# A macaron encoder block on one core: the feed-forward activations turned by DMA in 16-bit halves instead of by TensorE

## The chip, the cores and the metric

The kernel runs on one core of a Trainium2 chip. The metric is device time in microseconds of one execution of the whole program; lower is better. Inputs and weights lie in the chip's memory in a layout packed for the kernel, and packing is not timed.

## The reference, cut to what matters

```python
# x (1, 256, 2048), d_ff = 5632, everything float32
x = x + 0.5 * swiglu(rmsnorm(x, ffn1_norm), w_gate1, w_up1, w_down1)
h = rmsnorm(x, mix_norm)
z = h @ w_in                                   # 2048 -> 7168: u | v | gate logits
a = pool_branch(u); b = conv_branch(v)         # pooling and 31-tap convolution, each -> 2048
x = x + (sigmoid(g_a) * a + sigmoid(g_b) * b) @ w_out
x = x + 0.5 * swiglu(rmsnorm(x, ffn2_norm), w_gate2, w_up2, w_down2)
out = rmsnorm(x, final_norm)

def swiglu(h, w_gate, w_up, w_down):
    return (silu(h @ w_gate) * (h @ w_up)) @ w_down
```

The change touches only the product silu(...) * (...) of the two feed-forwards, on its way into `w_down`.

## The kernel before

All 256 tokens stay on the chip as two tiles `X` of 128 tokens by 2048. Weights stream from memory once, in pieces of 128 rows by 1024 columns (`raw`, five buffers), issued on SP's queue.

**Words in two parts.** TensorE multiplies in a shortened float32 format, so every operand is held as a high part and a low part: `hi_lo` lets ScalarE cast to the high part (`wh`, L153) and VectorE subtract it for the low part (`wl`, L155). A product is three matmuls: high by high, high weights' low part, low activations (L256).

**Chunks.** The work is one list, `stream`, of chunks. A chunk is two pieces of weights (256 rows of the inner dimension), and a `Unit` is the run of chunks that fills one set of accumulators: 8 chunks for a unit of 2048 rows. A normal chunk is 24 matmuls of 128x512. Chunks 0 and 2 of most feed-forward units (`SEVEN`) use a seven-product form instead: 21 matmuls, for which VectorE first forms sums of weights (`sum`, L193), ScalarE casts them (`exth`, L153) and VectorE subtracts (`extl`, L155).

**The order.** No scheduler reorders anything: `run` walks the list. At chunk i it issues the loads of chunk i+2, casts the weights of chunk i+1 (`split_chunk`), calls what was put down for this place with `at(i, ...)`, and then issues chunk i's matmuls (`run_chunk`). Each engine executes its own instructions in that order. Converted weights have buffers for two chunks.

**The feed-forward.** A gate unit multiplies by 512 columns of `w_gate` and 512 of `w_up` together; there are 11 such units in a feed-forward. After units 4 and 8 come the units of `w_down` for the four hidden blocks finished so far, and at the end those for the last three. When a gate unit's last chunk is issued, `gate_done_seven` (for unit 0 `gate_done`) adds the partial results on VectorE (`part`, L413), applies silu on ScalarE (L414) and multiplies on VectorE (`h`, L418): two tiles of 128 tokens by 512 hidden columns.

`w_down` needs the hidden columns on the partitions. So `put` has TensorE turn four 128x128 squares of h against an identity into one bank of PSUM (`transposes`, L343), and `hi_lo` makes the high and low parts of `ht` out of the bank. It is called twice for a unit, in chunks 4 and 5 of the next unit, with two 128-column blocks each time; `gate_early` puts it down there, `rest_of_hidden` after the last unit. For the chunks in the seven-product form a copy `hy` (L389) feeds `e_forms`, which makes differences of hidden blocks (`hE`).

Of the kernel before, what the change touches and what calls it, by code (L numbers as in the profile page):

```python
# [7 lines left out]

F32 = mybir.dt.float32
F32R = mybir.dt.float32r  # L10
AF = mybir.ActivationFunctionType
ALU = mybir.AluOpType

P = 128
D = 2048
T = 256
NT = T // P
# [8 lines left out]
C = 512  # L26
W2 = 2 * C
KD = D // P
# [12 lines left out]
GROUP = 4  # L41
# [40 lines left out]
def encoder_kernel(ctx: ExitStack, tc: tile.TileContext, x, xT, vecs, rows, pool_m,  # L82
# [30 lines left out]
    def at(i, fn):  # L113

        side.setdefault(i, []).append(fn)
# [12 lines left out]
    def add_unit(u):  # L128
        for cc in range(u.k // 2):
            stream.append((u, cc))  # L130
# [21 lines left out]
    def hi_lo(src, h, l=None):  # L152
        nc.scalar.copy(out=h, in_=src)  # L153
        if l is not None:
            nc.vector.tensor_tensor(out=l, in0=src, in1=h.bitcast(F32), op=ALU.subtract)  # L155
        return h, l
# [136 lines left out]
    def hidden(pool, name):  # L293

        return [tuple(block(pool, f"h{s}{u}", F32R, f"{name}{s}{u}") for s in "hl") for u in range(GROUP)]

# [5 lines left out]
    def e_forms(dst, even, odd):  # L302

        e = stg.tile([P, 4, P], F32, tag="sg", name=f"e{Pos.now}")
        a11, a21, a12, a22 = even[:, :P], even[:, P:], odd[:, :P], odd[:, P:]
        for n, (a, b) in enumerate(((a11, a21), (a21, a22), (a11, e[:, 1, :]), (a12, e[:, 2, :]))):
            nc.vector.tensor_tensor(out=e[:, n, :], in0=a, in1=b, op=ALU.subtract)
        hi_lo(e, *dst)
# [29 lines left out]
    def transposes(src_of, n, name, b=None):  # L338

        b = bank(name) if b is None else b  # L340
        for j in range(n):
            for t in range(NT):
                nc.tensor.transpose(out=b[:, j * T + t * P: j * T + (t + 1) * P],  # L343
                                    in_=src_of(j, t), identity=ident)
        return b
# [24 lines left out]
    def open_ffn(stack, n):  # L370

        pool = ffn["pool"] = stack.enter_context(tc.tile_pool(name=f"ffn{n}", bufs=1))
        ffn["ht"] = hidden(pool, f"ht{n}")
        ffn["hE"] = e_tiles(pool, "h", n)
        ffn["t0"], ffn["t1"] = (pool.tile([P, 2, C], F32, tag=f"part{t}", name=f"part{n}_{t}") for t in range(NT))

    def ffn_units(w_g, w_d, xt, xE, rs, residual_done, tail=None):
        waiting = []

        def hidden_lhs(k, t):  # L380
            return tuple(h[:, k % 4, t * P:(t + 1) * P] for h in ffn["ht"][k // 4])

        def put(u, hs, k0, b=None):
            b = transposes(lambda j, t: hs[t][:, (k0 + j) * P:(k0 + j + 1) * P], 2, f"hT{Pos.now}_{k0}", b)
            hi_lo(b.rearrange("p (q t) -> p q t", q=2), *(h[:, k0:k0 + 2, :] for h in ffn["ht"][u % GROUP]))
            c = (u % GROUP) * 2 + k0 // 2
            if c in SEVEN:
                y = stg.tile([P, 2, T], F32, tag="sg", name=f"hy{Pos.now}_{k0}")
                nc.scalar.copy(out=y, in_=b.rearrange("p (q t) -> p q t", q=2))  # L389
                e_forms(ffn["hE"][c], y[:, 0, :], y[:, 1, :])  # L390

        def hidden_tile(t):
            return stg.tile([P, C], F32, tag="h", name=f"h{Pos.now}_{t}")

        def gate_done(u):
            def done(acc):
                hs = []
                for t in range(NT):
                    sg = stg.tile([P, C], F32, tag="sg", name=f"sg{Pos.now}_{t}")
                    h = hidden_tile(t)  # L400
                    nc.scalar.activation(sg, acc[t][:, 0, :], AF.Silu, scale=rs[:, t:t + 1])  # L401
                    nc.vector.scalar_tensor_tensor(out=h, in0=acc[t][:, 1, :], scalar=rs[:, t:t + 1],
                                                   in1=sg, op0=ALU.mult, op1=ALU.mult)
                    hs.append(h)
                waiting.append((u, hs))
            return done

        def gate_done_seven(u):
            def done(acc):
                hs = []  # L410
                for t in range(NT):
                    z = ffn[f"t{t}"]
                    nc.vector.tensor_tensor(out=z, in0=acc[t], in1=z, op=ALU.add)  # L413
                    nc.scalar.activation(z[:, 0, :], z[:, 0, :], AF.Silu, scale=rs[:, t:t + 1])  # L414
                for t in range(NT):
                    z = ffn[f"t{t}"]
                    h = hidden_tile(t)
                    nc.vector.scalar_tensor_tensor(out=h, in0=z[:, 1, :], scalar=rs[:, t:t + 1],  # L418
                                                   in1=z[:, 0, :], op0=ALU.mult, op1=ALU.mult)
                    hs.append(h)  # L420
                waiting.append((u, hs))
            return done

        def shared_parts():

            z0, z1 = ffn["t0"], ffn["t1"]
            nc.scalar.copy(out=z0[:, 0, :], in_=ps[:, B_P1, :])
            for out, a, b, op in ((z1[:, 1, :], ps[:, B_P6, :], z0[:, 0, :], ALU.subtract),
                                  (z0[:, 1, :], ps[:, B_P5, :], z1[:, 1, :], ALU.add),
                                  (z1[:, 0, :], ps[:, B_P7, :], z1[:, 1, :], ALU.subtract),  # L430
                                  (z1[:, 1, :], z0[:, 1, :], ps[:, B_P7, :], ALU.subtract)):
                nc.vector.tensor_tensor(out=out, in0=a, in1=b, op=op)

        def gate_early():
            shared_parts()
            if waiting:
                u, hs = waiting.pop()
                at(Pos.now + 1, lambda: put(u, hs, 0, ps[:, B_P6, :]))
                at(Pos.now + 2, lambda: put(u, hs, 2, ps[:, B_P1, :]))

        def into_residual(t, half, part):
            xs = X[t][:, half * W2:(half + 1) * W2]
            nc.vector.scalar_tensor_tensor(out=xs, in0=part.rearrange("p a b -> p (a b)"), scalar=0.5, in1=xs,
                                           op0=ALU.mult, op1=ALU.add)

        def down_early(half):
            def early():
                shared_parts()
                for t in range(NT):
                    at(Pos.now + 1 + t, lambda t=t: into_residual(t, half, ffn[f"t{t}"]))  # L450
            return early

        def down_done(half, last):
            def done(acc):
                for t in range(NT):
                    into_residual(t, half, acc[t])
                    if last:
                        squares(t, 2 * half, half * W2, (half + 1) * W2)
                if last:
                    residual_done(half)  # L460
            return done

        def rest_of_hidden():
            u, hs = waiting.pop()
            at(Pos.now + 2, lambda: put(u, hs, 0))
            at(Pos.now + 3, lambda: put(u, hs, 2))

        def add_down(g, k, last):
            for half in range(2):
                if last:  # L470
                    add_unit(Unit(w_d[half], k, hidden_lhs, down_done(half, True), tail if half else None,
                                  k0=g * GROUP * 4, start=None if half else rest_of_hidden))
                else:
                    add_unit(Unit(w_d[half], k, hidden_lhs, down_done(half, False), k0=g * GROUP * 4,
                                  forms=forms_of(hidden_lhs, LateE()), early=down_early(half), seven=SEVEN))

        class LateE:
            def __getitem__(self, c):
                return ffn["hE"][c]

        units = FF // C
        for u in range(units):
            if u:
                add_unit(Unit(w_g[u], KD, lhs_of(xt), gate_done_seven(u), forms=forms_of(lhs_of(xt), xE),
                              early=gate_early, seven=SEVEN, start=(lambda: None) if u == 1 else None))
            else:
                add_unit(Unit(w_g[u], KD, lhs_of(xt), gate_done(u)))
            if u and u % GROUP == 0:
                add_down(u // GROUP - 1, 4 * GROUP, False)
        add_down((units - 1) // GROUP, 4 * (units - (units - 1) // GROUP * GROUP), True)  # L490
# [387 lines left out]
    at(n3 - 1, final_first_half)  # L878


    xr = [block(ffn["pool"], f"xr{j}", F32, f"xr{j}") for j in range(4)]
    start()
    for i in range(PF - 1):
        load(i)
# [124 lines left out]
```

## Time and profile before

| what | value |
|---|---|
| median of 3 runs | 1945.61 us (1945.37 to 1945.71) |
| the profiled execution's own time | 1945.58 us |
| its span in the profile | 1943.8 us |
| granted TensorE clock | 0.999 |
| memory read | 380.28 MB, 197 GB/s over the span |

All rows below come from that one execution. "Busy" is the time in which an engine had an instruction under way. The chain that ended last goes back from the last instruction, at each step to what released it, and says which engine set the end. In rows in order of time the first number is the start in microseconds from the span's start and the second the duration; square brackets hold the engine's idle time before the row and what ended it. ACTq stands for ScalarE's instruction queue issuing a DMA, SPq for SP's.

### The profile page before, as it was taken

What the parts mean: (1) busy time and instruction counts of PE and PEld (TensorE: products, weight loads), DVE (VectorE), ACT (ScalarE), POOL (GpSimd) and SP (SyncE); (2) the same over time, 40 slices, a digit from 0 to 9 for tenths busy, and PEclk for the clock granted to TensorE, in tenths of its full rate; (3) what the DMA queues carried; (4) which work ended last, traced back from release to release, by engine and by line L of the source; (5) the groups of instructions that cost most, each with busy time, mean ns of one, the idle gap of its engine ahead of it and who ended that gap; (6) DMA issues with size and microseconds to landing.
All of it is one profiled execution on the core that took longest, in us unless ns stands there. A gap on an engine that the chain in (4) does not pass through costs nothing.

```text
span 1943.8 us, 23272 instructions
## 1 busy us (share of the span) xinstructions
PE 1931.8 (99%) x8680; PEld 1597.5 (82%) x8680; DVE 1520.0 (78%) x1762; ACT 975.7 (50%) x1117; POOL 11.3 (1%) x22
## 2 busy tenths in 40 slices
PE   9999999999999999999999999999999999999998
PEld 7888888888888888888888888888888888888886
DVE  6888888888888555888888766688888888888855
ACT  6555544554545454454444545455554455554544
POOL 0000000000000000000000000000000000000000
PEclk9999999999999999999999999999999999999999
DMA  8555566655665556566666555555656665566664
GB/s 316 191 183 198 193 216 192 203 190 190 198 204 201 189 188 202 189 200 208 204 206 200 190 184 185 183 194 179 201 196 215 191 199 193 186 201 203 197 194 147
DMA packets 106145, 383.90 MB, mean 198 GB/s; under 512 B 11920, under 2 KB 12176, under 8 KB 105776
## 3 DMA queue, kind: packets, MB, share of 16 engines
q1 hardware_dynamic: 104688, 378.45, 59.2%
q0 software_dynamic: 1056, 3.83, 0.6%
q8 instruction: 68, 1.11, 0.2%
q14 instruction: 45, 0.37, 0.1%
q10 hardware_dynamic: 288, 0.14, 0.0%
HBM read 380.28 MB, written 2.10 MB: 197 GB/s over the span
## 4 chain that ended last, share of the span: by engine, by line
PE 98%; DVE 1%; issue 0%; ACT 0%; DMA 0%; DVEq 0%; POOLq 0%; POOL 0%; ACTq 0%
PE ps L256 82%; PE ps L277 13%; PE ps L343 2%; PE ps L741 0%; DVE wl L155 0%; DMA xr<-in_xT 0%; DVE sum L193 0%; PE ps L716 0%; ACT exth L153 0%; ACT wh L153 0%; DVE extl L155 0%; DVE raw L193 0%; ACT fsq L850 0%; ACT sg L401 0%; PE ps L623 0%
## 5 line engine op out<-in xcount | busy, mean ns | idle before, releaser
L153 ACT CAST wh<-raw 128x1024 fp32r<-128x1024 f32 (+1 forms) x706 | 726.5, 1048 | 710.9 <-PE ps L256 393.9
L155 DVE TENSOR_TENSOR wl<-raw,wh 128x1024 fp32r<-128x1024 f32 (+1 forms) x706 | 844.5, 1218 | 300.4 <-ACT wh L153 297.4
L256 PE MATMUL ps<-wh,xt1h 128*128 128x512 f32 x544 | 170.6, 395 | 1.2 <-ACT wh L153 1.2
L256 PE MATMUL ps<-wh,xt3h 128*128 128x512 f32 x544 | 169.6, 393 | 0.0
L256 PE MATMUL ps<-wl,xt1h 128*128 128x512 f32 x544 | 168.4, 391 | 0.0
L256 PE MATMUL ps<-wh,xt1l 128*128 128x512 f32 x544 | 168.0, 390 | 0.0
L256 PE MATMUL ps<-wl,xt3h 128*128 128x512 f32 x544 | 167.9, 390 | 0.0
L256 PE MATMUL ps<-wh,xt3l 128*128 128x512 f32 x544 | 167.6, 389 | 0.0
L256 PE MATMUL ps<-wh,xt2h 128*128 128x512 f32 x448 | 138.4, 390 | 0.0
L256 PE MATMUL ps<-wl,xt2h 128*128 128x512 f32 x448 | 138.1, 389 | 0.0
L256 PE MATMUL ps<-wh,xt2l 128*128 128x512 f32 x448 | 137.9, 389 | 0.0
L256 PEld LDWEIGHTS ps<-wl,xt1h 128*128 128x128 f32 x544 | 102.6, 189 | 21.9 <-DVE wl L155 0.3
L256 PEld LDWEIGHTS ps<-wh,xt1l 128*128 128x128 f32 x544 | 102.4, 188 | 21.6
L256 PEld LDWEIGHTS ps<-wh,xt3l 128*128 128x128 f32 x544 | 102.1, 188 | 21.7
L256 PEld LDWEIGHTS ps<-wl,xt3h 128*128 128x128 f32 x544 | 102.1, 188 | 21.5
L256 PEld LDWEIGHTS ps<-wh,xt1h 128*128 128x128 f32 x544 | 101.1, 189 | 21.4 <-ACT wh L153 1.7
L155 DVE TENSOR_TENSOR extl<-sum,exth 128x1536 fp32r<-128x1536 f32 x56 | 98.5, 1759 | 25.4 <-ACT exth L153 25.4
L256 PEld LDWEIGHTS ps<-wh,xt3h 128*128 128x128 f32 x544 | 100.5, 188 | 19.5
L256 PEld LDWEIGHTS ps<-wl,xt2h 128*128 128x128 f32 x448 | 84.1, 188 | 17.7
L256 PEld LDWEIGHTS ps<-wh,xt2l 128*128 128x128 f32 x448 | 84.1, 188 | 17.5
L600 DVE SCALAR_TENSOR_TENSOR conv<-gluT,vec,conv 128x241 f32<-128x241 f32 (+14 forms) x240 | 96.9, 471 | 0.0
L256 PEld LDWEIGHTS ps<-wh,xt2h 128*128 128x128 f32 x448 | 83.3, 188 | 16.5
(237 smaller groups left out, 2851.9 us busy)
## 6 DMA issues: line engine op xcount, KB each, us to landing
raw<-in_w_g SPq DMA_DIRECT2D x350, 512.0 KB, 4.2
raw<-in_w_d SPq DMA_DIRECT2D x176, 512.0 KB, 4.0
raw<-in_w_in SPq DMA_DIRECT2D x112, 512.0 KB, 3.9
raw<-in_w_out SPq DMA_DIRECT2D x32, 512.0 KB, 3.5
raw<-in_w_pp SPq DMA_DIRECT2D x16, 512.0 KB, 3.7
raw<-in_w_cp SPq DMA_DIRECT2D x16, 512.0 KB, 3.8
row<-in_rows POOLq DMA_DIRECT2D x7, 512.0 KB, 4.0
X<-in_x SPq DMA_DIRECT2D x2, 1024.0 KB, 8.7
```

Source lines behind the costliest of these rows:

```text
L153: nc.scalar.copy(out=h, in_=src)
L155: nc.vector.tensor_tensor(out=l, in0=src, in1=h.bitcast(F32), op=ALU.subtract)
L256: nc.tensor.matmul(u.acc[t + c if u.tail and t else t][:, c, :], lhsT=a, rhs=b[:, c * C:(c + 1) * C], start=(t, c) not in u.begun, stop=k ...
L277: nc.tensor.matmul(ps[:, b, :], lhsT=x_, rhs=w_, start=where not in u.begun, stop=b < B_11 and cc == u.seven[-1] and n == 2)
L343: nc.tensor.transpose(out=b[:, j * T + t * P: j * T + (t + 1) * P], in_=src_of(j, t), identity=ident)
L600: nc.vector.scalar_tensor_tensor(out=dst, in0=src, scalar=w, in1=dst, op0=ALU.mult, op1=ALU.add)
```

## The change

Each h tile is turned by two steps in place of one. `turn`, in the first chunk of the next unit: ScalarE copies h, seen as 16-bit words, into `halves`, the low halves of all words first and then the high ones, and its queue issues a DMA that transposes the 128x1024 half-words into `turned`, eight squares of 128x128. That is done for both token tiles. `put`, in chunk 4 of the next unit: ScalarE joins the halves again with four copies into `y`, and `hi_lo` works on `y`, all four blocks at once. `e_forms` follows one chunk later. The buffers of `ht` are allocated only once the first unit has run, since `xr`, the transposed input, now lies in some of them.

```diff
+U16 = mybir.dt.uint16
 ...
+        def open_hidden():
+            ffn["ht"] = hidden(ffn["pool"], f"ht{stream.index((first, 0))}")
 ...
-        def put(u, hs, k0, b=None):
-            b = transposes(lambda j, t: hs[t][:, (k0 + j) * P:(k0 + j + 1) * P], 2, f"hT{Pos.now}_{k0}", b)
-            hi_lo(b.rearrange("p (q t) -> p q t", q=2), *(h[:, k0:k0 + 2, :] for h in ffn["ht"][u % GROUP]))
-            c = (u % GROUP) * 2 + k0 // 2
-            if c in SEVEN:
-                y = stg.tile([P, 2, T], F32, tag="sg", name=f"hy{Pos.now}_{k0}")
-                nc.scalar.copy(out=y, in_=b.rearrange("p (q t) -> p q t", q=2))
-                e_forms(ffn["hE"][c], y[:, 0, :], y[:, 1, :])
+        def turn(u, hs):
+            turned = []
+            for t in range(NT):
+                halves = ffn["pool"].tile([P, 2, C], U16, tag=f"halves{t}", name=f"halves{Pos.now}_{t}")
+                nc.scalar.copy(out=halves, in_=hs[t].bitcast(U16).rearrange("p (f w) -> p w f", w=2))
+                z = ffn["pool"].tile([P, 8, P], U16, tag=f"turned{t}", name=f"turned{Pos.now}_{t}")
+                nc.scalar.dma_start_transpose(out=z, in_=halves.rearrange("p w f -> p (w f)"))
+                turned.append(z)
+            waiting.append((u, turned))
+
+        def put(u, turned):
+            y = ffn["pool"].tile([P, 4, T], F32, tag="y", name=f"hy{Pos.now}")
+            whole = y.bitcast(U16).rearrange("p j (t w) -> p w j t", w=2)
+            for t in range(NT):
+                for w in range(2):
+                    nc.scalar.copy(out=whole[:, w, :, t * P:(t + 1) * P], in_=turned[t][:, 4 * w:4 * w + 4, :])
+            hi_lo(y, *ffn["ht"][u % GROUP])
+            for c in SEVEN:
+                if c // 2 == u % GROUP:
+                    q = c % 2 * 2
+                    at(Pos.now + 1, lambda c=c, q=q: e_forms(ffn["hE"][c], y[:, q, :], y[:, q + 1, :]))
 ...
-                waiting.append((u, hs))
+                at(Pos.now + 1, lambda: turn(u, hs))
 ...
-                u, hs = waiting.pop()
-                at(Pos.now + 1, lambda: put(u, hs, 0, ps[:, B_P6, :]))
-                at(Pos.now + 2, lambda: put(u, hs, 2, ps[:, B_P1, :]))
+                u, turned = waiting.pop()
+                at(Pos.now + 1, lambda: put(u, turned))
 ...
         def rest_of_hidden():
-            u, hs = waiting.pop()
-            at(Pos.now + 2, lambda: put(u, hs, 0))
-            at(Pos.now + 3, lambda: put(u, hs, 2))
+            at(Pos.now + 3, lambda: put(*waiting.pop()))
 ...
-    xr = [block(ffn["pool"], f"xr{j}", F32, f"xr{j}") for j in range(4)]
+    xr = [block(ffn["pool"], f"h{x}{j}", F32, f"xr{x}{j}") for j in (2, 3) for x in "hl"]
```

The order of instructions at the three places that matter, in the stretch where unit 2 of the first feed-forward has ended (chunk 23) and unit 3 runs (chunks 24 to 31). The number in a name is the chunk it belongs to. First ScalarE at the start of unit 3, before the change (the two silus of unit 2, the weights of chunk 25, the three casts of chunk 26):

```order
L414 ACTIVATE part1_0_115<-part1_0_115,rstd0_82 128x512
L414 ACTIVATE part1_1_116<-part1_1_116,rstd0_82 128x512
L153 CAST wh25_0_1226<-raw25_0_1169 128x1024
L153 CAST wh25_1_1230<-raw25_1_1171 128x1024
L153 CAST wh26_0_1266<-raw26_0_1222 128x1024
L153 CAST exth26_1264<-sum26_1259 128x1536
L153 CAST wh26_1_1272<-raw26_1_1224 128x1024
```

And now:

```order
L432 ACTIVATE part1_0_107<-part1_0_107,rstd0_82 128x512
L432 ACTIVATE part1_1_108<-part1_1_108,rstd0_82 128x512
L154 CAST wh25_0_1228<-raw25_0_1171 128x1024
L154 CAST wh25_1_1232<-raw25_1_1173 128x1024
L391 COPY halves24_0_1236<-h23_0_1220 128x1024
L393 DMA_TRANSPOSE turned24_0_1238<-halves24_0_1236 128x8x128
L391 COPY halves24_1_1240<-h23_1_1222 128x1024
L393 DMA_TRANSPOSE turned24_1_1242<-halves24_1_1240 128x8x128
L154 CAST wh26_0_1276<-raw26_0_1224 128x1024
L154 CAST exth26_1274<-sum26_1269 128x1536
L154 CAST wh26_1_1282<-raw26_1_1226 128x1024
```

Two copies and two DMA issues stand between the casts of chunk 25 and those of chunk 26. The second place is ScalarE at chunks 20 and 21, where the activations of unit 1 (turned at chunk 16) become `ht`; before the change:

```order
L153 CAST ht1h1_105<-ps_87 128x512
L389 COPY hy20_0_1058<-ps_87 128x512
L153 CAST hEh2_1_113<-e20_1060 128x512
L153 CAST wh22_0_1095<-raw22_0_1040 128x1024
L153 CAST wh22_1_1099<-raw22_1_1042 128x1024
L153 CAST ht1h1_105<-ps_87 128x512
```

And now:

```order
L403 COPY hy20_1061<-turned16_0_903 128x4x128 x2
L403 COPY hy20_1061<-turned16_1_907 128x4x128 x2
L154 CAST ht0h1_559<-hy20_1061 128x1024
L154 CAST wh22_0_1096<-raw22_0_1049 128x1024
L154 CAST wh22_1_1100<-raw22_1_1051 128x1024
L154 CAST hEh2_1_105<-e21_1104 128x512
```

The work on `ht` has become one block of five ScalarE instructions in chunk 20, and the cast of the differences has moved behind the weights of chunk 22. The third place is TensorE between chunks 27 and 28, before the change (two more rows like the last two follow, and then chunk 28):

```order
L256 MATMUL ps_87<-wh27_1_1308,xt1h1_90 128x512 x2
L256 MATMUL ps_87<-wl27_1_1309,xt1h1_90 128x512 x2
L256 MATMUL ps_87<-wh27_1_1308,xt1l1_91 128x512 x2
L343 MATMUL ps_87<-ident_75,h23_0_1218 128x128
L343 MATMUL ps_87<-ident_75,h23_1_1220 128x128
```

And now:

```order
L257 MATMUL ps_87<-wh27_1_1318,xt1h1_90 128x512 x2
L257 MATMUL ps_87<-wl27_1_1319,xt1h1_90 128x512 x2
L257 MATMUL ps_87<-wh27_1_1318,xt1l1_91 128x512 x2
L257 MATMUL ps_87<-wh28_0_1347,xt1h2_92 128x512 x2
L257 MATMUL ps_87<-wl28_0_1348,xt1h2_92 128x512 x2
```

The transposes between the two chunks are gone; the matmuls around them are as they were.

More of the change, by code (lines that the diff above doesn't have):

```diff
@@ L372, in open_ffn @@
         pool = ffn["pool"] = stack.enter_context(tc.tile_pool(name=f"ffn{n}", bufs=1))
-        ffn["ht"] = hidden(pool, f"ht{n}")
         ffn["hE"] = e_tiles(pool, "h", n)
@@ L420, in done @@
                     hs.append(h)
-                waiting.append((u, hs))
+                at(Pos.now + 1, lambda: turn(u, hs))
             return done
@@ L486, in ffn_units @@
             else:
-                add_unit(Unit(w_g[u], KD, lhs_of(xt), gate_done(u)))
+                first = Unit(w_g[u], KD, lhs_of(xt), gate_done(u))
+                add_unit(first)
+                at(len(stream), open_hidden)
             if u and u % GROUP == 0:
```

## The prediction

> **What bounds the kernel now.** I read the page's first part, then the chain that ended last, then the chain again inside one feed-forward unit, then each engine's rows in order of time there.
>
> ```profile
> PE 1931.8 (99%) x8680; PEld 1597.5 (82%) x8680; DVE 1520.0 (78%) x1762; ACT 975.7 (50%) x1117; POOL 11.3 (1%) x22
> PE ps L256 82%; PE ps L277 13%; PE ps L343 2%; PE ps L741 0%; DVE wl L155 0%; DMA xr<-in_xT 0%; DVE sum L193 0%; PE ps L716 0%; ACT exth L153 0%; ACT wh L153 0%; DVE extl L155 0%; DVE raw L193 0%; ACT fsq L850 0%; ACT sg L401 0%; PE ps L623 0%
> ...
> 139.62 4.76 PE ps L277 x21
> 144.38 5.44 PE ps L256 x24
> 149.82 4.85 PE ps L277 x21
> 154.67 5.44 PE ps L256 x24
> 160.12 0.44 PE ps L343 x4
> 160.55 5.50 PE ps L256 x24
> ...
> L343 PE MATMUL ps<-ident,h x176: 270/272/273, 73.5 to 1885.3; 128*128 128x128 f32 x176
> ```
>
> TensorE is the chain: 98% of the span, with no holes, so every TensorE instruction taken out shortens the run, and every late operand lengthens it. The stretch from 139.62 is unit 3 of the first feed-forward: chunks 24 (seven-product form, x21), 25 (x24), 26 (x21), 27 (x24), then a group of four transposes of unit 2's activations. These are the L343 rows that the change deletes.
>
> ScalarE is busy for half of the span, but where it stands in that stretch matters more (start, duration, engine, line, instruction, the idle time before it with its cause):
>
> ```profile
> 139.53 0.73 ACT L414 ACTIVATE part<-part,rstd 128x512 f32<-128x512 f32 x1 [3.15 <-DVE part L413]
> 140.92 0.72 ACT L414 ACTIVATE part<-part,rstd 128x512 f32<-128x512 f32 x1 [0.66 <-DVE part L413]
> 141.55 1.98 ACT L153 CAST wh<-raw 128x1024 fp32r<-128x1024 f32 x2
> 146.47 1.05 ACT L153 CAST wh<-raw 128x1024 fp32r<-128x1024 f32 x1 [2.94 <-DVE raw L193]
> 147.87 1.49 ACT L153 CAST exth<-sum 128x1536 fp32r<-128x1536 f32 x1 [0.34 <-DVE sum L193]
> 149.26 3.89 ACT L153 CAST wh<-raw 128x1024 fp32r<-128x1024 f32 x4
> ...
> 160.15 1.06 ACT L153 CAST wh<-raw 128x1024 fp32r<-128x1024 f32 x1 [1.67 <-PE ps L256]
> 161.12 0.57 ACT L153 CAST ht1h<-ps 128x512 fp32r<-128x512 f32 x1
> 163.41 1.05 ACT L153 CAST wh<-raw 128x1024 fp32r<-128x1024 f32 x1 [1.72 <-issue]
> ...
> 140.80 1.63 DVE L418 SCALAR_TENSOR_TENSOR h<-part,rstd 128x512 f32<-128x512 f32 x2
> 147.67 1.22 DVE L155 TENSOR_TENSOR wl<-raw,wh 128x1024 fp32r<-128x1024 f32 x1
> 149.39 1.76 DVE L155 TENSOR_TENSOR extl<-sum,exth 128x1536 fp32r<-128x1536 f32 x1 [0.50 <-ACT exth L153]
> ...
> 151.01 0.39 PE L277 MATMUL ps<-exth,xEh 128*128 128x512 f32 x1
> 151.24 0.46 PE L277 MATMUL ps<-extl,xEh 128*128 128x512 f32 x1
> 151.54 0.39 PE L277 MATMUL ps<-exth,xEl 128*128 128x512 f32 x1
> ```
>
> The two silus, then chunk 25's casts (end 143.53), then 2.94 us of idling until VectorE has prepared chunk 26's words, then chunk 26's three casts. VectorE's extl ends at 151.15, and TensorE wants it at 151.24: there it steps 0.30 us where its steps around are 0.23. Chunk 26's chain exth, extl, matmul has no slack at all. The 2.94 us of idling is the only cover there.
>
> **The change part by part.** *Transposes leave TensorE.* A group costs 0.44 us, and the chunk behind it takes 5.50 where one without takes 5.44: 0.50 us. 176 of them are 44 groups: 22.0 us off the chain, two groups in each of 22 units.
>
> *ScalarE and VectorE, in sum.* Leaving ScalarE in each unit: two 128x512 casts from PSUM (0.57). Coming: two 128x1024 copies that split, four 128x512 that join, one 128x1024 cast. No row shows a copy of 16-bit halves at a stride. By element count it is 1.05 for 1024 and 0.58 for 512 (the cast rows); half of that if half-words move twice as fast, double if a stride costs one step more. I take the cast rows, since the count of elements is the same. That is 2.1+2.3+1.05 in, 1.15 out: +4.3 us, times 22 = +95, so about 1070 of 1950 us: not the bound on average. VectorE trades two subtractions for one of 1.22: nothing, under its 78%.
>
> *The joining copies (`put`)* stand behind chunk 29's cast, 161.2 to about 164.8. The next cast, 163.41 before, slides by 1.4 us, but its words are first used in chunk 30, some 8 us later; the cover is the operand buffers of two chunks. Zero. They wait for the transposed data; that is safe if it lands by 161, some 12 us after the issue.
>
> ```profile
> raw<-in_w_g SPq DMA_DIRECT2D x350, 512.0 KB, 4.2
> out_y<-X SPq DMA_DIRECT2D x8, 256.0 KB, 3.0
> q1 hardware_dynamic: 104688, 378.45, 59.2%
> 139.46:182.66 43.20, 43.20 (x195) 35.61 (x194) 35.24 (x37) 21.98 (x23) 0.00 (x0) 1.00 0.59 195
> ```
>
> A transfer of 256 KB lands in 3.0 us here, so I cost landing at zero. Moving e_forms one chunk later costs nothing: its users stand in the down projection, a whole unit or more away. On SP nothing is added; weight loads come behind a transpose only by sharing the 16 DMA engines (rival C).
>
> *The splitting copies and the issues (`turn`)* stand just between chunk 25's casts and chunk 26's: in the hole of 2.94 us. h is ready at 142.43, before they start. A transposing DMA does not occur in this trace. The ScalarE queue's own DMAs are the nearest rows:
>
> ```profile
> 0.75 0.41 ACTq L510 DMA_DIRECT2D vec<-in_vecs  x1
> 1.19 0.45 ACTq L515 DMA_DIRECT2D xr<-in_xT  x1
> 1.67 1.28 ACT L512 ACT_TABLE_LOAD   x1 [1.67 <-PEq L998]
> ```
>
> An issue holds the engine: the next instruction begins only when both are over. 8 KB take 0.41, 128 KB 0.45, so bytes hardly count. Let t be the time one transposing issue holds ScalarE. Low end: it is one more DMA, t = 0.45. High end: its output is 128x8x128, eight squares, and each is issued like a DMA of its own, 8 x 0.45 = 3.6. Less than 0.41 no row supports. The operation is neither row: a plain issue hands over 128 rows as they lie, this one must address eight squares turned. I take the middle, 2.0.
>
> Now the hole: copy 143.43 to 144.48, issue t, copy 1.05, issue t, with about 0.05 at each hand-over: chunk 26's first cast may begin at 145.7 + 2t. It began at 146.47, and exth could follow 0.95 later without delay if it began by 146.9. So up to 2t = 1.2 is hidden, and beyond that TensorE waits 2t - 1.2 for extl in every unit. Behind the issues stand all casts, and VectorE's subtractions wait for these; nothing catches it up, since chunk 26 needs them at once. 0.6 us each would be free; at t = 2.0 it is 2.8 us. Ten of eleven units in each feed-forward have such a seven-product unit behind them: 20 x 2.8 = 56. The last unit is followed by plain chunks with about 1.5 us more slack: 1 us, twice, 2.
>
> Sum on the profiled execution (its time 1945.58, span 1943.8; the median of the runs is 1945.61, the same): 1945.6 - 22 + 56 + 2 = 1982 us. Even is 20 x (2t - 1.2) = 22, t = 1.15 us. Ends: t = 0.45 gives 1945.6 - 22 = 1924; t = 3.6 gives -22 + 20 x 6.0 + 2 x 4 = +106, 2052. Splitting copies at half or double price move the sum by -21 or +42.
>
> [...]
>
> **The rivals.**
>
> *A, faster: the issue is one DMA like any other.* For it: the ACTq rows, whose length does not follow the bytes. Against it: none of them rearranges anything. Condition: t under 1.05. Then the copies and the issues fit into the hole, the TensorE saving stands alone, and the time is 1924 (up to 1942 as t nears 1.05). [...]
>
> *B, much slower: the issue is longer than eight plain ones.* [...] For it: only that the page of the profile prices no such thing; against: none of the queues' rows is above 0.45 on this engine.
>
> *C, slower: the DMA engines become the bound.* 256-byte pieces, 1024 to a transpose. If each holds an engine as long as a 3.6 KB packet of the q1 row (0.592 x 1943.8 x 16 / 104688 = 0.176 us), a transpose takes 1024 x 0.176 / 16 = 11.3 us of all 16, two 22.5. A unit's window has 0.59 x 43.2 = 25.5 of its own; together 48.0, against 43.2. Over 22 units +106: 2051. Against it: small pieces should cost less than large ones, and the five raw buffers hold two and a half chunks, 13 us, against 4.2 for a load. It decides from about 0.13 us for a piece.
>
> **How the numbers follow.** Chances: the forecast (t from 1.25 to 3.6) 0.53, A 0.25, break-even between them 0.05, C 0.10, B 0.07. The time is the forecast's, 1982; its own range is 1950 to 2052. A takes the range down to 1922, and part of the double-priced copies and of C up to 2060. What lies within 0.2% (3.9 us) is what a measurement of this kernel cannot tell from no change. Faster 0.25, same 0.05, slower 0.70.
>
> **What would show it.** No L343 rows with h; chunks follow at 5.44. On ACTq, 44 DMA_TRANSPOSE rows: their duration is t, and decides. If I am right, chunk 26's first cast starts late, released by nothing but the issue, and TensorE shows holes of about 2.8 us ahead of its exth or extl matmuls, once in each unit, and none elsewhere. Holes ahead of chunk 28 or at the joining copies would mean late landing (C); a DMA share near 1 likewise. Copies of half-words far from 1.05 and 0.58 would move the sum without touching its form. I am wrong if t is below 1.15, or if ScalarE goes on while an issue is under way.

## The result, and the profile after

The changed kernel takes 1963.49 us (median of 4 runs, 1962.17 to 1965.29) against 1945.66 before: a ratio of 1.0092, 95% interval 1.0075 to 1.011. It is slower by 17.8 us, where +36 was forecast. The profiled execution took 1962.23 us with a span of 1960.4, 16.7 more than before.

From the page of the changed kernel: busy time, the chain that ended last by engine, the two hardware queues. Then, from the answers on the tile `turned` and on groups of instructions: the issues (nanoseconds minimum/median/maximum) and their landing, and the copies of half-words (busy us, mean ns).

```profile
PE 1924.6 (98%) x8504; PEld 1579.2 (81%) x8504; DVE 1517.1 (77%) x1740; ACT 1065.3 (54%) x1215; POOL 11.3 (1%) x22
PE 83%; ACT 6%; DVE 4%; DMA 3%; issue 2%; ACTq 2%; DVEq 0%; POOLq 0%; POOL 0%
q1 hardware_dynamic: 104688, 378.45, 58.6%
q10 hardware_dynamic: 46752, 11.68, 8.1%
L393 ACTq DMA_TRANSPOSE turned<-halves x44: 1247/1284/2375, 56.8 to 1890.3; - x44
DMA to landing us min/median/max: 7.5/10.0/12.4
L391 ACT COPY halves<-h 128x1024 uint16<-128x1024 uint16 x44 | 45.9, 1043 | 29.1 <-DVE sum L194 26.5 <-DVE wl L156 2.6
L403 ACT COPY hy<-turned 128x512 uint16<-128x512 uint16 x88 | 58.4, 765 | 0.0
```

TensorE no longer is the whole chain: 15 points of it have gone to ScalarE, VectorE, DMA and the issues. The unknown t is there: 1.28 us, neither the 0.45 of a plain DMA nor the assumed 2.0. The data lands after 10.0 us, not 3; still, none of the 88 joining copies waited for it.

The chain around the end of a unit of the changed kernel (unit 3 of the first feed-forward, chunk 32 begins at about 186), in order of time, then TensorE's rows there:

```profile
189.43 1.99 ACT wh L154 x2
191.42 0.95 ACT halves L391
192.37 0.02 issue
192.39 1.25 ACTq L393
193.64 0.04 issue
193.68 1.06 ACT halves L391
194.74 0.02 issue
194.76 1.44 ACTq L393
...
197.27 1.48 ACT exth L154
198.75 0.02 issue
198.77 1.77 DVE extl L156
200.54 0.04 issue
200.59 3.51 PE ps L278 x14
...
197.54 0.39 PE L278 MATMUL ps<-wh,xt1h 128*128 128x512 f32 x1
198.68 0.50 PE L278 MATMUL ps<-wl,xt1h 128*128 128x512 f32 x1 [0.75 <-DVE wl L156]
199.02 0.39 PE L278 MATMUL ps<-wh,xt1l 128*128 128x512 f32 x1
...
199.94 0.40 PE L278 MATMUL ps<-exth,xEh 128*128 128x512 f32 x1
200.59 0.50 PE L278 MATMUL ps<-extl,xEh 128*128 128x512 f32 x1 [0.24 <-DVE extl L156]
```

This is the forecast mechanism: casts of the first chunk's successor, copy, issue, copy, issue, and only then the casts of the second seven-product chunk; extl ends at 200.54 and TensorE steps 1.14 us ahead of wl's matmul to the next and 0.65 ahead of extl's, instead of 0.23. (The brackets count only the idle time after the end of the matmul before.)

To see where all of the time went, compare the start of every chunk's first matmul in the two traces. A chunk's difference in length, summed by place (so that matmuls that themselves ran slower are in it too):

| us against the kernel before | transposes gone | holes at the first chunks of the 20 units with a seven-product unit behind | last units (2) | rest | sum |
|---|---|---|---|---|---|
| forecast | -22 | +56 | +2 | 0 | +36 |
| changed kernel | -20.9 | +32.8 | +4.4 | +0.7 | +17.1 |

Of the 20 units, 17 have a hole of 1.38 to 1.55 us; three in the first feed-forward have 2.4 to 3.1. "Hole" means this whole difference of one unit from here on.

### The profile page after: what moved, and what is told of

The parts are those of the page before. It is cut to its first block, busy times and chain, and to the rows that moved or that the text cites. A ratio compares the mean times of both kernels' runs of the same rounds, so it can differ in the third digit from the quotient of the medians.

```text
span 1960.4 us, 23002 instructions
## 1 busy us (share of the span) xinstructions
PE 1924.6 (98%) x8504; PEld 1579.2 (81%) x8504; DVE 1517.1 (77%) x1740; ACT 1065.3 (54%) x1215; POOL 11.3 (1%) x22
## 3 DMA queue, kind: packets, MB, share of 16 engines
q10 hardware_dynamic: 46752, 11.68, 8.1%
## 4 chain that ended last, share of the span: by engine, by line
PE 83%; ACT 6%; DVE 4%; DMA 3%; issue 2%; ACTq 2%; DVEq 0%; POOLq 0%; POOL 0%
PE ps L257 73%; PE ps L278 9%; ACT wh L154 2%; DMA raw<-in_w_g 2%; ACTq L393 2%; DVE extl L156 2%; ACT exth L154 2%; ACT halves L391 1%; DMA raw<-in_w_d 1%; DVE wl L156 1%; PE ps L344 1%; ACT hy L403 0%; PE ps L758 0%; DVE part L431 0%; DMA xrh<-in_xT 0%
```

## The experiments

Theory H: the holes are the time for which issues hold ScalarE between the casts of two chunks. Rival L: they come from late landing, of weights beside a transpose or of the turned data. Rival S: what is saved on ScalarE is lost on SP.

**Issue from SP.** The whole change, but one word:

```diff
-                nc.scalar.dma_start_transpose(out=z, in_=halves.rearrange("p w f -> p (w f)"))
+                nc.sync.dma_start_transpose(out=z, in_=halves.rearrange("p w f -> p (w f)"))
```

> The changed kernel with the 44 transposes issued from SP's queue; ScalarE keeps only the splitting and joining copies. Theory H (ScalarE's hold): what the change loses is the 2 x 1.3 us that the issues hold ScalarE between the casts of two chunks (some 33 of +38 us of TensorE holes). Off ScalarE these holes close and the removed transposes (-21) show: about 1930, at most 1935, with holes left only at the end of each feed-forward. Rival L (late landing): the holes come from weight loads that land in 9 to 10 us beside a transpose, and from the data landing after 10 us; the issuing queue does not matter: about 1960 as in the changed kernel. Rival S: SP, held 2.6 us and waiting for the copies in front of its weight loads, delays them, and new holes for weights appear: 1940 to 1960.

Measured: 1925.50 us (1924.43 to 1926.13), ratio to before 0.9896, interval 0.9881 to 0.9911. Its rows on `turned`, ScalarE in order of time around chunk 24 (the place shown ahead of the prediction) and the chain there; then what ScalarE's casts waited for, in this run and, last, in the changed kernel (us in total, times, longest):

```profile
L393 SPq DMA_TRANSPOSE turned<-halves x44: 1237/1312/2112, 56.4 to 1854.6; - x44
DMA to landing us min/median/max: 3.1/3.2/4.9
...
139.70 1.99 ACT L154 CAST wh<-raw 128x1024 fp32r<-128x1024 f32 x2
141.59 1.99 ACT L391 COPY halves<-h 128x1024 uint16<-128x1024 uint16 x2
144.62 1.06 ACT L154 CAST wh<-raw 128x1024 fp32r<-128x1024 f32 x1 [1.04 <-DVE raw L194]
146.02 1.48 ACT L154 CAST exth<-sum 128x1536 fp32r<-128x1536 f32 x1 [0.34 <-DVE sum L194]
...
137.77 4.76 PE ps L278 x21
142.53 5.44 PE ps L257 x24
147.97 4.87 PE ps L278 x21
...
ACT wh L154 <- DMA raw<-in_w_g: 32.5, 63, 2.2
ACT wh L154 <- DMA raw<-in_w_d: 21.5, 22, 4.0
...
ACT wh L154 <- DMA raw<-in_w_g: 44.4, 33, 3.3
ACT wh L154 <- DMA raw<-in_w_d: 19.6, 12, 3.2
```

The two copies fit into the hole and leave 1.04 us of it; TensorE is back to 4.76, 5.44, 4.87 with no holes. By place: transposes -20.9, the 20 units 0.0, last units +0.7. The time is near the one that H gives. SP is held as long (1.31 us an issue), and before the first issue of a unit it waits some 10 us for the copy (218.5 us in 22 waits); ScalarE then waits for weights 85 times, more often than the 45 times in the changed kernel. But TensorE shows no hole for it, so S is there and hidden, and late weights alone do not make the holes. One thing this run leaves open: with the queue the landing changed too (3.2 us in place of 10.0), so it does not part H from L in the transposes' own landing. This version beats both kernels.

**The issues alone, on ScalarE and on SP.** The kernel before with its TensorE transposes (and `ht`, `xr` allocated as in the changed kernel), plus an unused copy and transpose in the place of `turn`:

```diff
+        def turn(hs):
+            for t in range(NT):
+                halves = ffn["pool"].tile([P, 2, C], U16, ...)
+                nc.scalar.copy(out=halves, in_=hs[t].bitcast(U16).rearrange("p (f w) -> p w f", w=2))
+                z = ffn["pool"].tile([P, 8, P], U16, ...)
+                nc.scalar.dma_start_transpose(out=z, ...)      # the other run: nc.sync
 ...
+                at(Pos.now + 1, lambda: turn(hs))
```

> The kernel before, TensorE transposes kept and used, with the splitting copies and the 44 transposing DMAs of the changed kernel added on ScalarE in the same place; their result is not used. Theory H: holes of about 1.45 us in 20 units and nothing at the last units: 1945.6 + 30 = 1975, up to 1980 with loads that land late. Rival L, in the form that the joining copies' waiting for data makes the holes: 1946 to 1950, since nothing waits for the data here.

> The same as the run before with the unused transposes issued from SP's queue: the transfers' competition with the weight loads, without the hold of ScalarE. Theory H: 1946 to 1949. Rival L (weight loads delayed by transfers make the holes): as much as with ScalarE's issue, 1960 to 1975.

Measured: from ScalarE 1977.49 us (ratio 1.0163, 1.0146 to 1.018), from SP 1945.21 (ratio 1.0, 0.999 to 1.0009). What TensorE waited for, ScalarE's issue first, then SP's (us in total, times, longest):

```profile
PE ps L278 <- DVE wl L156: 12.3, 19, 0.8
PE ps L278 <- DVE extl L156: 6.8, 20, 1.3
...
PE ps L278 <- DVE extl L156: 0.2, 1, 0.2
PE ps L278 <- DVE wl L156: 0.2, 1, 0.2
```

The same bytes and copies: holes of 33.5 us in the 20 units with ScalarE's issue (1.30 to 2.74 each), -0.2 with SP's, none at the last units, where nothing here waits for the data. So the holes are not the copies' either, which both runs have, and they need nobody who waits for the turned data. (The landing differs in this pair as well, 10.1 us against 3.2.)

**A plain DMA in the same place.** The first of these two runs with

```diff
-                nc.scalar.dma_start_transpose(out=z, in_=halves.rearrange("p w f -> p (w f)"))
+                nc.scalar.dma_start(out=z.rearrange("p b c -> p (b c)"), in_=halves.rearrange("p w f -> p (w f)"))
```

> The kernel before, TensorE transposes kept, with the splitting copies and, in the place of the unused transposes, 44 plain DMAs of the same bytes from the one buffer to the other, issued on ScalarE. A plain issue of 0.41 to 0.45 us: 2 x 0.45 = 0.9 us is under the 1.2 us that the hole hides, so no hole on TensorE: 1945 to 1948. If any DMA issued there costs what the transposes did, 1975.

Measured: 1945.36 us (ratio 0.9998, 0.9989 to 1.0008). Its row:

```profile
L400 ACTq DMA_DIRECT2D turned<-halves x44: 472/472/506, 56.1 to 1874.3; - x44
```

Two holds of 0.47 us, 0.94 together, stay under the free 1.2 and are hidden. Rival A of the prediction was right about plain issues; a transposing issue, 1.28 us in the changed kernel, is not a plain one.

**Twice as many issues of half the size.**

```diff
+                for w in range(2):
+                    nc.scalar.dma_start_transpose(out=z[:, 4 * w:4 * w + 4, :], in_=halves[:, w, :])
```

> The changed kernel with each transpose issued as two of half the size, 128x512 half-words, 88 instructions. If the hold follows the squares: 0.63 us each, the same 2.6 us in a unit, 1963. If an instruction has a fixed part of 0.45 us like a plain DMA and 0.10 us a square: 0.85 each, 3.4 us in a unit, +0.8 us in 20 units, about 1980. If it is all fixed: 1.3 each, 5.2 in a unit, +2.6 in 20 units, about 2015.

**One issue of twice the size** (both token tiles in one buffer, `z` of 16 squares):

```diff
+            nc.scalar.dma_start_transpose(out=z, in_=halves.rearrange("p t w f -> p (t w f)"))
+            turned = [z[:, 8 * t:8 * t + 8, :] for t in range(NT)]
```

> The changed kernel with both token tiles split into one buffer and turned by one DMA of 128x2048 half-words, 22 issues on ScalarE instead of 44. If an issue holds the engine for a fixed 1.25 to 1.3 us whatever its size: chunk 26's first cast could begin at 145.7 + 1.3 = 147.0, 0.1 us too late at most, the holes of 1.45 us close, and about 1927 to 1932 is left with late data at the last units. If the hold grows with the squares above eight: 2.5 us for one issue, the holes stay, 1960 to 1965.

Measured: 2033.45 us for half the size (ratio 1.0452, 1.0431 to 1.0474), 1980.98 for twice the size (1.0183, 1.0166 to 1.02). Their issue rows, in that order, ScalarE in order of time at the end of two neighbouring units of the second, and how long its casts waited for gate weights in all of the second run:

```profile
L394 ACTq DMA_TRANSPOSE turned<-halves x88: 1204/1285/2240, 56.6 to 1965.9; - x88
L392 ACTq DMA_TRANSPOSE turned<-halves x22: 1332/4209/5219, 57.0 to 1906.8; - x22
...
150.52 4.07 ACTq L392 DMA_TRANSPOSE turned<-halves  x1
154.71 1.04 ACT L154 CAST wh<-raw 128x1024 fp32r<-128x1024 f32 x1 [4.22 <-issue]
...
195.48 1.33 ACTq L392 DMA_TRANSPOSE turned<-halves  x1
196.93 1.05 ACT L154 CAST wh<-raw 128x1024 fp32r<-128x1024 f32 x1 [1.48 <-DVE raw L194]
...
ACT wh L154 <- DMA raw<-in_w_g: 3.5, 4, 1.5
```

Four squares hold the engine as long as eight, 1.2 to 1.3 us at the median: up to eight squares the hold is the instruction's, not the squares'. Sixteen are worse than both outcomes that were expected: 3.9 to 5.2 us in 17 units and 1.33 in five, each fourth one; why is open.

But that split is a test inside one trace, and it parts H from L. The data lands alike in all units, 6.0 to 7.2 us after the issue, and ScalarE waited for gate weights four times in 3.5 us, as in the kernel before (four times, 3.9 us). In the five units with a hold of 1.33 the holes are -0.04, -0.03, 0.00, 0.00 and 0.01 us; the unit with 4.07 has 2.7. A hold of 1.33 us in all is hidden (a free time of 1.2 would leave 0.1 of it), one of 4.1 is not, and no cast waits for late weights here.

The run with four issues a unit holds 4 x 1.25 + 0.1; the rule gives 5.1 - 1.2 = 3.9. Four of its units have 3.85 to 3.95, the other 16 have 4.85 to 6.9. The surplus over the rule, some 27 us in the 20 units, is TensorE's clock: right after the wait in each of these 16 the granted clock is 0.5 for 3.4 or 6.8 us, and matmuls that take 0.39 us elsewhere take 0.63. That costs some 32 us, 5 of them in place of waiting. From the answer on stretches of time (start:end, length, busy us of PE, PEld, DVE, ACT and POOL with the number of instructions, granted clock, DMA share, GB/s), after the wait in a unit with 6.9 us and in one with 3.95:

```profile
254.60:261.40 6.80, 6.26 (x14) 4.59 (x15) 6.59 (x6) 5.19 (x6) 0.00 (x0) 0.50 0.57 176
207.50:210.90 3.40, 2.36 (x8) 1.46 (x9) 3.25 (x3) 3.40 (x4) 0.00 (x0) 1.00 0.74 206
```

The length of the wait alone does not tell when the clock falls: it did not after waits of 3.9 us here, and it did after one of 1.6 us in the changed kernel (below). No run tests what does.

**The same two issues, apart.** The second tile's copy and issue one chunk later, behind the casts that were late:

```diff
+            one(0)
+            at(Pos.now + 1, lambda: one(1))
```

> The changed kernel with the same 44 issues on ScalarE, but the second token tile is split and issued one chunk later, behind chunk 26's casts. If only the place of the hold counts (2.94 us of idle time ahead of chunk 26's casts, a chunk's work more of room behind them): the first copy and issue take 2.4 us of the 2.94, the second pair pushes chunk 27's casts by 2.4 us to within 0.2 us of their use: 1926 to 1934. If each microsecond of hold on ScalarE costs wherever it stands: as the changed kernel, 1963.

Measured: 1956.67 us (ratio 1.0062, 1.0046 to 1.0078): a miss of over 20 us, in another place. By place: -20.9, the 20 units 14.0 instead of 32.8, and the two last units 17.8 instead of 4.4. ScalarE at the end of the first feed-forward:

```profile
672.94 1.40 ACT L406 COPY hy<-turned 128x512 uint16<-128x512 uint16 x2
681.08 1.38 ACT L406 COPY hy<-turned 128x512 uint16<-128x512 uint16 x2 [6.75 <-DMA turned<-halves]
```

Fourteen of the 20 units have at most 0.4 us, as H says; six carry the rest, and whether late weights or the hold make it there is not separated (one has an issue of 2.92 us). But issued later and landing up to 18 us after the issue, the data of the last unit is not there when `w_down` needs it: here L is right, for the data.

**One issue of twice the size, from SP.** The 128x2048 run with `nc.sync`.

> One transpose of 128x2048 for a unit, issued from SP: 22 issues. From SP nothing waited with 44 issues (1925.5), so halving them should change nothing: 1924 to 1927. If SP's hold of its weight loads still costs something: 1 to 3 us less than 1925.5.

Measured: 1926.69 us (ratio 0.9906, 0.9891 to 0.992). The 20 units have 0.2 us of holes. The profiled execution, at 1930.36 us the slowest of the four, has 5.1 at the last units, where a cast waited 6.2 us for weights whose loads stand behind the transpose in SP's order: there S has a part. Fewer issues gain nothing once they are off ScalarE.

## Why the prediction was right or wrong

*The mechanism* was right: the place (the second seven-product chunk), the cause (issues that keep ScalarE from the casts), the free 1.2 us, once in each of 20 units. Unit by unit, the two measured holds less 1.2 us give the hole to within 0.1 us in 18 of the 20; a typical unit has 1.25 + 1.28 to 1.44. One detail differs: the chain was drawn through exth and extl, but two thirds of TensorE's wait fall a few matmuls earlier, at wl (13.1 us in all, 6.9 at extl), behind the same late cast. The run with plain issues shows that 0.94 us are free, the run from SP that without the hold there is no hole.

*The step that failed is t*, "I take the middle, 2.0": 1.28 us at the median, 1.34 in the mean. The middle of two bounds eightfold apart carried the whole of the sum. The argument for the high end, one plain issue for each square, is refuted up to eight squares: four take as long as eight. With the measured holds the term is 30 us in place of 56, and that of the last units (1.5 us more of slack) is nothing in place of 2: -22 + 30 = +8.

*What the sum then lacks*, about 9 us of the 17 in the table, it had nearly all at nothing. The one row in question, landing, was read for the wrong transfer: "a transfer of 256 KB lands in 3.0 us here, so I cost landing at zero" is about the turned data, which took 10.0 and still kept no copy waiting. What came late was weights. A load issued 0.5 us behind a transpose landed after 8 to 12 us, and in the last unit the joining copies stand behind a cast that waited for one. TensorE's wait at the end of the second feed-forward (us in total, times, longest), then ScalarE there:

```profile
PE ps L257 <- ACT ht222h L154: 2.4, 1, 2.4
...
1902.48 1.05 ACT L154 CAST wh<-raw 128x1024 fp32r<-128x1024 f32 x1 [2.67 <-DMA raw<-in_w_d]
1903.43 2.63 ACT L403 COPY hy<-turned 128x512 uint16<-128x512 uint16 x4
1906.09 1.04 ACT L154 CAST ht222h<-hy 128x1024 fp32r<-128x1024 f32 x1
```

At the end of the first feed-forward a cast in the same place waited 2.77 us for its weights. This makes the +4.4 us of the last units. Of the three large units, one (2.43) is the hold itself: its second issue took 2.38 us. The first (3.1) has 1.6 us of waiting, as its holds give, and 1.5 of slow matmuls: from 66.1 us on the granted clock is 0.50 for 3.4 us. The third (2.49) has 1.1 us more than its holds give; its silus begin 1.5 us after the chunk's first matmul in place of 0.1, and in the unit before it ScalarE waited 3.25 and 1.54 us for weights, so late weights are the likely cause, argued and not shown. The rest is 1.1 us that the transposes saved less, and 0.7 in no one place. So the number came as near as it did by luck: a hold sized too long stood in for waits and a clock that the sum did not have.

*The transposes* were sized well: 22.0 forecast, 20.9 measured, and the run from SP shows that all of it comes out when nothing else is late. *The copies*: splitting 1.04 us as assumed; joining 0.67 (four in 2.67 us) instead of 0.58, hidden as said.

*Rival A* put 1924 on issues short enough to be hidden, and 1925.5 was measured with ScalarE free, by another queue rather than a short issue. *Rival C* is refuted as a bound: 46752 packets took 8.1% of the engines, 0.081 x 1960.4 x 16 / 46752 = 0.054 us for a piece, under the 0.13 at which it would have decided. *Rival B* did not occur at eight squares; at sixteen, most issues on ScalarE pass the 3.6 us of eight plain ones.

## What to carry to other kernels

The instruction that issues a DMA occupied the engine it is written on here, 0.47 us plain and 1.28 turned, and that time counted like arithmetic: put it on a queue whose engine has slack at that place, and look at what stands behind it there. Ask of an engine's idle time not its share but which gap the new work must fit, and what waits at the gap's end: half-idle ScalarE had 2.94 us there, and what went beyond the gap and its little slack went nearly one to one into the time. When one unmeasured number carries the sum, neighbouring rows bound it but do not place it; state the break-even (here 1.15 us) first. When an unexplained surplus is left, look at the granted clock behind the waits before calling it open.

## What the runs showed of the hardware

A transposing issue of 1024 half-words a row holds its engine for 1.28 us at the median on ScalarE and 1.31 on SP (single ones take up to 2.4, and 2.9 in the run with the issues apart); at 512 it is 1.29 on ScalarE; a plain one of the same bytes as the first takes 0.47. At 2048 it is 1.65 to 2.85 on SP and 1.33 or 3.9 to 5.2 on ScalarE.

With the queue the landing changed: 3.2 us behind the weight loads on their own queue (plain stores of 256 KB from SP landed after 3.0), 10.0 on the other one, for the same transposes (the two unused-transpose runs agree: 3.2 and 10.1). In the changed kernel a weight load issued 0.5 us after a transpose landed with it, some 10 us later; with both on SP's queue the load behind a transpose landed 3.3 to 5.2 us after its own issue. The queue is not all of it: plain DMAs of the same bytes on ScalarE's queue, with a load as close behind, landed after 6.1 us; transposes of twice the size there, beside which no load was issued in the first 3.7 us, landed after 6.4. The plain DMAs' queue moved its 11.68 MB in 6624 packets, the transposes' queue the same 11.68 MB in 46752, and in 46048 at twice the size. What delays the landing, no run tested by itself.

TensorE's granted clock fell to 0.5 for 3.4 or 6.8 us right after the waits of 16 of the 20 units in the run with four issues a unit, of five in the run with 2048 half-words from ScalarE and of one in the changed kernel; matmuls of 128x512 then took 0.63 us in place of 0.39.
